# A decoder block's up projection: one 512-column matmul for both parts of x, and banks emptied ahead of weight splits

## The chip, the cores and the metric

The kernel runs on one core of a Trainium2 chip. The metric is the device time of one execution in microseconds (us). Three runs of the kernel before gave 404.71, 404.85 and 405.25 us; the median is 404.85 us.

## What is computed

One decoder block on 256 tokens of width 1024 in float32. The first half normalises x, projects it to q, k, v, an SSM input and two gates, runs attention and a state space model, mixes them and adds the result to x. The second half, where the change lies, is a squared-ReLU MLP:

```python
h = rms_norm(x, norm_mlp_g)
x = x + jnp.square(jax.nn.relu(h @ w_up)) @ w_down    # w_up 1024 x 4096, w_down 4096 x 1024
return rms_norm(x, norm_final_g)
```

## The kernel before, in words

Each float32 operand of a matmul is split in two parts: hi, a copy rounded to the type `F32R`, and lo, the remainder, which is rounded to the same type. A product is then three matmuls, hi·xh, hi·xl and lo·xh; `mm3` (L87 to L90) writes them out. `split` (L82) makes the parts: ScalarE (ACT) writes hi with a copy (L83), VectorE (DVE) writes lo with a subtraction (L84).

Weights come from HBM in units of 128 rows by 1024 columns, 512 KB each. `w_unit` (L73) takes a unit's DMA buffer (tag "raw", 5 buffers) and splits it into tags "hi" and "lo" (4 buffers each). The split is made under a scheduling priority raised by `SPLIT_PRIO` = 800. A planner orders each engine's instructions before the run: what does not depend on each other may change places, and a raised priority lets an instruction go ahead of others that are ready.

The order of stages is: projections, attention and SSM; the GLU (tile `glu`); the output projection (tile `wo`, L676 to L695); the up projection (tile `up`, L705 to L721); the down projection (tiles `dn` and `dnq`, L728 to L796); the final norm.

In the stage `wo`, x is the stationary operand and 512 columns of weights are streamed. It runs over two halves of the channels, c = 0 and 1. Behind each half, DVE adds the residual (L687), TensorE (PE) transposes the result into tile `xt` (L689), ACT writes `x2h` (L693) and DVE writes `x2l` (L694), one 128-channel slice k at a time. Slices k = 0 to 3 come from c = 0, slices 4 to 7 from c = 1.

In the up projection the weights are the stationary operand and the 256 tokens are streamed. One `w_up` unit yields 128 output channels from eight slices k. `up_pair(i)` takes two units, and fills the two halves of one PSUM bank with 2 x 8 x 3 matmuls of 256 columns. It then empties the bank with a Relu on ACT (L714), squares on DVE (L715), and splits the square into `hh` and `hl` (L83 and L84). There are 16 pairs, thus 32 units and 768 matmuls. The banks come from `mm_bank`, a set of three. In the first pair the loop runs over k outside and over the two units inside, in the others the reverse.

Between the two stages, L696 to L699 form the sums of squares of the new x on ACT and turn them into `st2` on DVE. Those are read first by the down projection's `residual` (L739).

Of the kernel before, what the change touches and what calls it, by code (L numbers as in the profile page):

```python
# [8 lines left out]
F32 = mybir.dt.float32  # L9
F32R = mybir.dt.float32r  # L10
BF16 = mybir.dt.bfloat16
I32 = mybir.dt.int32
AF = mybir.ActivationFunctionType
ALU = mybir.AluOpType
PSUM = bass.MemoryType.PSUM

P = 128
D = 1024
T = 256
KD = D // P  # L20
# [3 lines left out]
FF = 4096  # L24
EPS = 1e-6
# [11 lines left out]
SPLIT_PRIO = 800  # L37
HEAT = 7
RSP = 600
ATT_PRIO = 300  # L40
LAST = 4
WQ = (256, 256)
# [6 lines left out]
def build(ctx, tc, dr, out):  # L49
    nc = tc.nc  # L50
    V, S, G, PE = nc.vector, nc.scalar, nc.gpsimd, nc.tensor

    keep = ctx.enter_context(tc.tile_pool(name="keep", bufs=1))
# [4 lines left out]
    def bank(tag, bufs, name):  # L58
        return ps.tile([P, 2, T], F32, tag=tag, bufs=bufs, name=name)

    def mm_bank(name):
        return bank("mm", 3, name)
# [5 lines left out]
    def w_load(src, name):  # L68
        raw = keep.tile([P, 1024], F32, tag="raw", bufs=RAW, name=f"raw_{name}")
        nc.sync.dma_start(raw, src)  # L70
        return raw

    def w_unit(src, name, raw=None):  # L73
        if raw is None:
            raw = w_load(src, name)
        hi = keep.tile([P, 1024], F32R, tag="hi", bufs=HI, name=f"hi_{name}")
        lo = keep.tile([P, 1024], F32R, tag="lo", bufs=LO, name=f"lo_{name}")
        with tc.high_priority(SPLIT_PRIO):
            split(hi, lo, raw)
        return hi, lo  # L80

    def split(hi, lo, x):  # L82
        ins = S.copy(hi, x).ins  # L83
        V.tensor_sub(lo, x, hi.bitcast(F32))  # L84
        return ins

    def mm3(o, wh, wl, xh, xl, first, last, **kw):  # L87
        PE.matmul(o, wh, xh, start=first, stop=False, **kw)  # L88
        PE.matmul(o, wh, xl, start=False, stop=False, **kw)  # L89
        PE.matmul(o, wl, xh, start=False, stop=last, **kw)  # L90
# [28 lines left out]
    for c in range(4):  # L119
# [3 lines left out]
        for k2 in range(2):  # L123
            half = slice(k2 * 512, (k2 + 1) * 512)
# [28 lines left out]
        PE.matmul(hot, heat[:, 0:P], heat, start=True, stop=True)  # L153


    xgh = keep.tile([P, KD, T], F32R, tag="xh", name="xgh")
    xgl = keep.tile([P, KD, T], F32R, tag="xl", name="xgl")
    sq = p1.tile([P, KD, T], F32, tag="yhl", name="sq")
    u_acc = ps.tile([P, 2, 2, T], F32, tag="x", name="u_acc")
    for c in range(4):  # L160
        wh = keep.tile([P, 1024], F32R, tag="hi", bufs=HI, name=f"hi_u{c}")
        wl = keep.tile([P, 1024], F32R, tag="lo", bufs=LO, name=f"lo_u{c}")
        for k2 in range(2):
            k, cols = 2 * c + k2, slice(k2 * 512, (k2 + 1) * 512)
# [12 lines left out]
            ws = [slice(k2 * 512 + m * P, k2 * 512 + (m + 1) * P) for m in range(4)]  # L177
            for i, (w, x) in enumerate(((wh, xgh), (wh, xgl), (wl, xgh))):
                for m in range(4):
                    PE.matmul(u_acc[:, m // 2, m % 2, :], w[:, ws[m]], x[:, k, :],  # L180
                              start=(k == 0 and i == 0 and m % 2 == 0),
                              stop=(k == KD - 1 and i == 2), skip_group_check=True)
# [8 lines left out]
    def rsqrt(eng, dst, m, tmp):  # L191
        V.tensor_scalar(tmp.bitcast(I32), m.bitcast(I32), 1, None, op0=ALU.logical_shift_right)
        V.tensor_scalar(dst.bitcast(I32), tmp.bitcast(I32), -1.0, 1597463007.0,
                        op0=ALU.mult, op1=ALU.add)
        eng.tensor_scalar(m, m, -0.5, None, op0=ALU.mult)
        for _ in range(3):
            eng.tensor_mul(tmp, dst, dst)
            eng.tensor_mul(tmp, tmp, m)
            eng.tensor_scalar(tmp, tmp, 1.5, None, op0=ALU.add)
            eng.tensor_mul(dst, tmp, dst)  # L200

    ms = att_bank("ms")
    for h in range(2):
        for i in range(2):
            PE.matmul(ms[:, 0, h : h + 1], sq[:, i, h * P : (h + 1) * P], ones,
                      start=(i == 0), stop=(i == 1))
# [3 lines left out]
    rs_half = p1.tile([P, 2], F32, name="rs_half")  # L210
    with tc.high_priority(RSP):
        rsqrt(G, rs_tok, rsm[:, 0:2], rsm[:, 4:6])
    V.tensor_scalar(rs_half, rs_tok, 0.5, None, op0=ALU.mult)
    rs_ps = att_bank("rs_ps")
    for h in range(2):
        PE.matmul(rs_ps[:, 0, h * P : (h + 1) * P], rs_tok[:, h : h + 1].to_broadcast([P, P]),
                  ident, start=True, stop=True)
# [52 lines left out]
    def flat(x):  # L270
        return x.rearrange("p a b -> p (a b)")
# [32 lines left out]
    def attn_head(q, k, j):  # L304
        s = att_bank("s").rearrange("p a b -> p (a b)")
        PE.matmul(s[:, 0:128], q[:, j, 0:128], k[:, j, 0:128], start=True, stop=False,
                  skip_group_check=True)
        PE.matmul(s[:, 0:128], ident_b, tri_b, start=False, stop=True, skip_group_check=True)
        PE.matmul(s[:, 128:384], q[:, j, 128:256], k[:, j, :], start=True, stop=False,
                  skip_group_check=True)  # L310
        PE.matmul(s[:, 256:384], ident_b, tri_b, start=False, stop=True, skip_group_check=True)
        st = p1.tile([P, 6], F32, tag="st", bufs=2, name="st")
        V.tensor_reduce(st[:, 0:1], s[:, 0:128], axis=mybir.AxisListType.X, op=ALU.max)
        V.tensor_reduce(st[:, 1:2], s[:, 128:384], axis=mybir.AxisListType.X, op=ALU.max)
        V.tensor_scalar(st[:, 0:2], st[:, 0:2], -scale, None, op0=ALU.mult)
        pr = p1.tile([P, 384], F32, tag="pr", bufs=2, name="pr")
        act(pr[:, 0:128], s[:, 0:128], AF.Exp, bias=st[:, 0:1], scale=scale,
                     accum_out=st[:, 2:3])
        act(pr[:, 128:384], s[:, 128:384], AF.Exp, bias=st[:, 1:2], scale=scale,
                     accum_out=st[:, 3:4])  # L320
        V.reciprocal(st[:, 4:6], st[:, 2:4])
        S.activation(pr[:, 0:128], pr[:, 0:128], AF.Copy, scale=st[:, 4:5])
        S.activation(pr[:, 128:384], pr[:, 128:384], AF.Copy, scale=st[:, 5:6])
        return pr
# [276 lines left out]
    for step in ORDER.split():  # L601
        part, n = step[0], int(step[1])
# [13 lines left out]
        elif part == "S":  # L616
            q, k = qk.pop(n)
            with tc.high_priority(ATT_PRIO):
                prs[n] = [attn_head(q, k, j) for j in range(2)]
# [3 lines left out]
        elif part == "A":  # L623
            with tc.high_priority(ATT_PRIO):
                attn_out(n, prs.pop(n), tha.pop(n))
# [4 lines left out]
        elif part == "B":  # L630
            for i in range(2):
                thb[2 * n + i] = p1.tile([P, 2, T], F32, tag=("cs", "sn")[n], bufs=4,
                                         name=f"thb{2 * n + i}")
# [6 lines left out]
    def wide_banks(name):  # L640
        b = ps.tile([P, 2, 2, T], F32, tag="x", name=name)
        return [flat(b[:, h]) for h in range(2)]

    for q in range(4):
        acc = wide_banks(f"glu{q}") if q % 2 else [flat(mm_bank(f"glu{q}{h}")) for h in range(2)]
        for kk_ in range(2):
            wh, wl = w_unit(dr["w_glu"][2 * q + kk_], f"glu{q}{kk_}")
            for k2 in range(2):
                k, w = 2 * kk_ + k2, slice(k2 * 512, (k2 + 1) * 512)
# [4 lines left out]
        for hf in range(2):  # L654
# [5 lines left out]
            for i in range(2):  # L660
# [3 lines left out]
                               op0=ALU.mult, op1=ALU.add)  # L664
# [4 lines left out]
    p2 = ctx.enter_context(tc.tile_pool(name="ph2", bufs=1))  # L669
    x2t = p2.tile([P, 2, D], F32, name="x2t")  # L670
    nc.sync.dma_start(x2t, dr["x"].rearrange("(h p) d -> p h d", p=P))
    sq2 = p2.tile([P, D], F32, name="sq2")
    st2 = p2.tile([P, 16], F32, name="st2")
    x2h = keep.tile([P, KD, T], F32R, tag="xh", name="x2h")
    x2l = keep.tile([P, KD, T], F32R, tag="xl", name="x2l")
    for c in range(2):  # L676
        acc = wide_banks(f"wo{c}") if c else [flat(mm_bank(f"wo{c}{h}")) for h in range(2)]
        for kk_ in range(4):
            wh, wl = w_unit(dr["w_out"][c, kk_], f"wo{c}{kk_}")
            for k2 in range(2):  # L680
                k, w = 2 * kk_ + k2, slice(k2 * 512, (k2 + 1) * 512)
# [9 lines left out]
        for i in range(4):  # L691
            m, tp = 4 * c + i, tps[i // 2][:, i % 2, :]
            S.activation(x2h[:, m, :], tp, AF.Copy, scale=g_mlp[:, m : m + 1])  # L693
            V.scalar_tensor_tensor(x2l[:, m, :], tp, g_mlp[:, m : m + 1],  # L694
                                   x2h[:, m, :].bitcast(F32), op0=ALU.mult, op1=ALU.subtract)  # L695
    for hf in range(2):  # L696
        S.activation(sq2, x2t[:, hf, :], AF.Square, accum_out=st2[:, hf : hf + 1])
    V.tensor_scalar(st2[:, 2:4], st2[:, 0:2], 1.0 / D, EPS, op0=ALU.mult, op1=ALU.add)
    V.reciprocal(st2[:, 4:6], st2[:, 2:4])  # L699


    hh = p2.tile([P, FF // P, T], F32R, name="hh")
    hl = p2.tile([P, FF // P, T], F32R, name="hl")

    def up_pair(i):  # L705
        acc = mm_bank(f"up{i}")
        ws = [w_unit(dr["w_up"][2 * i + j], f"up{i}{j}") for j in range(2)]
        for k, j in [(k, j) for k in range(KD) for j in range(2)] if i == 0 else \
                    [(k, j) for j in range(2) for k in range(KD)]:
            w = [x[:, k * P : (k + 1) * P] for x in ws[j]]  # L710
            mm3(acc[:, j, :], *w, x2h[:, k, :], x2l[:, k, :],
                k == 0 and (i > 0 or j == 0), k == KD - 1, skip_group_check=(i == 0))
        hr = p2.tile([P, 2, T], F32, tag="hr", bufs=2, name="hr")
        S.activation(hr, acc, AF.Relu)  # L714
        V.tensor_mul(hr, hr, hr)  # L715
        split(hh[:, 2 * i : 2 * i + 2, :], hl[:, 2 * i : 2 * i + 2, :], hr)

    gfin = p2.tile([P, D], F32, name="gfin")
    nc.scalar.dma_start(gfin, dr["gfin"].partition_broadcast(P))
    for i in range(16):  # L720
        up_pair(i)  # L721

    r2 = st2[:, 4:6]
    x3 = x2t
# [43 lines left out]
    for c in range(2):  # L768
        acc = [mm_bank(f"dn{c}{h}").rearrange("p a b -> p (a b)") for h in range(2 - c)]
# [110 lines left out]
```

## Time and profile before

| what | value |
|---|---|
| median of three runs | 404.85 us |
| the profiled execution | 405.1 us |
| its span, first to last instruction | 403.2 us |
| mean granted clock of TensorE, as a share of full speed | 0.995 |
| PE busy share of the span | 98% |
| up projection, first to last matmul | 214.5 to 307.8 us |

The profiled execution takes 1.9 us outside its span. The profile's page gives busy time by engine, then a strip of 40 slices of the span. PE is TensorE's matmuls, PEld its weight loads, DVE VectorE, ACT ScalarE. A matmul's duration overlaps that of the next one, so what a matmul costs in a dense stream is the distance from its start to the start of the next.

### The profile page before, as it was taken

To read this page: it belongs to the slowest core of one execution; us is meant where nothing else is said; L and a number is where in the kernel's file an instruction comes from. 1 tells how busy PE (TensorE), PEld (TensorE's weight loads), DVE (VectorE), ACT (ScalarE), POOL (GpSimd) and SP (SyncE) were. 2 spreads that over 40 slices of the span, in tenths; PEclk is the share of its full clock that TensorE was granted. 3 is DMA by queue.
4 is the path that set the end of the run, shared out by engine and by line. 5 is a ranking of instruction groups with operands and counts; after the bars stand their busy time and mean duration, and the time that the engine had idled before them with its cause. 6 is when DMAs were issued, how large, how long until landed. Compare 5 with 4: busy or idle time off the path is not lost.

```text
span 403.2 us, 6862 instructions
## 1 busy us (share of the span) xinstructions
PE 394.3 (98%) x2635; PEld 355.2 (88%) x2635; DVE 292.8 (73%) x520; ACT 225.9 (56%) x360; POOL 30.3 (8%) x39
## 2 busy tenths in 40 slices
PE   8999999999999999999999999999999999999993
PEld 5988898989899787888889999999999888889983
DVE  5999999999999994769748665656565443564425
ACT  6767977655276557945647645464546334353323
POOL 4151492000000000000000000000000000000000
PEclk9999999999999999999999999999999999999998
DMA  8994843354516252456486465554555565555202
GB/s 228 401 337 149 246 154 102 111 202 151 192 56 208 84 195 102 158 159 206 161 308 209 152 215 191 176 194 172 191 178 193 172 205 169 199 192 178 101 0 104
DMA packets 23199, 71.57 MB, mean 178 GB/s; under 512 B 2944, under 2 KB 5248, under 8 KB 23168
## 3 DMA queue, kind: packets, MB, share of 16 engines
q1 hardware_dynamic: 20144, 68.92, 50.6%
q10 hardware_dynamic: 3024, 2.23, 1.9%
q8 instruction: 20, 0.33, 0.3%
q14 instruction: 11, 0.09, 0.1%
HBM read 69.18 MB, written 1.05 MB: 174 GB/s over the span
## 4 chain that ended last, share of the span: by engine, by line
PE 84%; DVE 5%; DMA 4%; ACT 2%; POOL 2%; issue 1%; ACTq 1%; SPq 0%; DVEq 0%
PE up L89 8%; PE up L90 8%; PE up L88 8%; PE dn L735 6%; PE dn L734 6%; PE dn L733 6%; PE k L88 2%; PE k L89 2%; PE k L90 2%; PE gb L268 2%; PE gb L266 2%; PE gb L267 2%; PE glu L268 2%; PE glu L266 2%; PE dnq L733 2%; PE dnq L735 2%
## 5 line engine op out<-in xcount | busy, mean ns | idle before, releaser
L89 PE MATMUL up<-x2l,hi_up 128*128 128x256 f32 x256 | 72.5, 284 | 0.0
L90 PE MATMUL up<-x2h,lo_up 128*128 128x256 f32 x256 | 72.3, 283 | 0.0
L88 PE MATMUL up<-x2h,hi_up 128*128 128x256 f32 x256 | 71.8, 283 | 0.0
L84 DVE TENSOR_TENSOR lo_dn<-raw_dn,hi_dn 128x1024 fp32r<-128x1024 f32 x32 | 39.2, 1225 | 44.0 <-ACT hi_dn L83 44.0
L83 ACT CAST hi_dn<-raw_dn 128x1024 fp32r<-128x1024 f32 x32 | 33.5, 1048 | 51.6 <-PE dn L735 25.8
L84 DVE TENSOR_TENSOR lo_up<-raw_up,hi_up 128x1024 fp32r<-128x1024 f32 x32 | 38.8, 1223 | 27.7 <-ACT hi_up L83 27.7
L83 ACT CAST hi_up<-raw_up 128x1024 fp32r<-128x1024 f32 x32 | 33.3, 1046 | 39.2 <-PE up L89 18.5
L89 PEld LDWEIGHTS up<-x2l,hi_up 128*128 128x128 f32 x256 | 49.1, 192 | 0.2 <-DVE x2l L694 0.2
L90 PEld LDWEIGHTS up<-x2h,lo_up 128*128 128x128 f32 x256 | 49.1, 192 | 0.0
L88 PEld LDWEIGHTS up<-x2h,hi_up 128*128 128x128 f32 x256 | 48.9, 192 | 0.1
L734 PE MATMUL dn<-lo_dn,hh 128*128 128x512 f32 x96 | 38.0, 395 | 0.0
L735 PE MATMUL dn<-hi_dn,hl 128*128 128x512 f32 x96 | 38.0, 395 | 0.0
L733 PE MATMUL dn<-hi_dn,hh 128*128 128x512 f32 x96 | 37.9, 395 | 0.0
L735 PEld LDWEIGHTS dn<-hi_dn,hl 128*128 128x128 f32 x96 | 18.0, 188 | 4.2
L733 PEld LDWEIGHTS dn<-hi_dn,hh 128*128 128x128 f32 x96 | 18.0, 188 | 3.8
L734 PEld LDWEIGHTS dn<-lo_dn,hh 128*128 128x128 f32 x96 | 18.0, 188 | 3.7
L89 PE MATMUL g<-xgl,hi_g 128*128 128x256 f32 x64 | 18.8, 294 | 0.0
L88 PE MATMUL k<-xgh,hi_k 128*128 128x256 f32 x64 | 18.4, 287 | 0.0
L90 PE MATMUL q<-xgh,lo_q 128*128 128x256 f32 x64 | 18.3, 286 | 0.0
L90 PE MATMUL g<-xgh,lo_g 128*128 128x256 f32 x64 | 18.3, 286 | 0.0
L90 PE MATMUL k<-xgh,lo_k 128*128 128x256 f32 x64 | 18.3, 286 | 0.0
L89 PE MATMUL q<-xgl,hi_q 128*128 128x256 f32 x64 | 18.3, 285 | 0.0
(267 smaller groups left out, 1046.9 us busy)
## 6 DMA issues: line engine op xcount, KB each, us to landing
raw_up<-w_up SPq DMA_DIRECT2D x32, 512.0 KB, 3.4
raw_dn<-w_down SPq DMA_DIRECT2D x32, 512.0 KB, 3.3
raw_v<-w_in SPq DMA_DIRECT2D x8, 512.0 KB, 6.0
raw_q<-w_in SPq DMA_DIRECT2D x8, 512.0 KB, 3.8
raw_k<-w_in SPq DMA_DIRECT2D x8, 512.0 KB, 3.2
raw_g<-w_in SPq DMA_DIRECT2D x8, 512.0 KB, 4.2
raw_gb<-w_in SPq DMA_DIRECT2D x8, 512.0 KB, 3.8
raw_glu<-w_glu SPq DMA_DIRECT2D x8, 512.0 KB, 3.2
```

The costliest lines, as they stand in the source:

```text
L83: ins = S.copy(hi, x).ins
L84: V.tensor_sub(lo, x, hi.bitcast(F32))
L88: PE.matmul(o, wh, xh, start=first, stop=False, **kw)
L89: PE.matmul(o, wh, xl, start=False, stop=False, **kw)
L90: PE.matmul(o, wl, xh, start=False, stop=last, **kw)
L266: PE.matmul(acc, xh[:, k, rows], wh, start=first, stop=False)
L267: PE.matmul(acc, xh[:, k, rows], wl, start=False, stop=False)
L268: PE.matmul(acc, xl[:, k, rows], wh, start=False, stop=last)
L733: PE.matmul(acc, xh, wh[:, w], start=(k == 0), stop=False, skip_group_check=True)
L734: PE.matmul(acc, xh, wl[:, w], start=False, stop=False, skip_group_check=True)
L735: PE.matmul(acc, xl, wh[:, w], start=False, stop=(k == 31), skip_group_check=True)
```

## The change

The two parts of x, until now tiles of their own (`xgh` and `xgl` in the first half, `x2h` and `x2l` in the second), become the two halves of one tile, so that for one k both lie side by side as 512 columns. `up_pair` gives way to `up_group(first, n)`. For each unit and k, one 512-column matmul streams xh and xl through the same hi weights. It puts hi·xh into the first half of a bank and hi·xl into the second half. Eight 256-column matmuls lo·xh follow into the first half. So a unit has 16 matmuls in place of 24, and a bank of its own. To empty it, ACT copies the second half to SBUF and DVE adds the first half; both are put under a priority raised by 2500. For each two units DVE then does ReLU and square in one instruction, and the split into `hh` and `hl` stays. The first call takes three units with k outside and units inside; the other 29 take one unit. The sums of squares move from ahead of the stage to behind its seventh unit.

```diff
+LEAVE_PRIO = 2500
-    xgh = keep.tile([P, KD, T], F32R, tag="xh", name="xgh")
-    xgl = keep.tile([P, KD, T], F32R, tag="xl", name="xgl")
+    xg = keep.tile([P, KD, 2, T], F32R, tag="xhl", name="xg")
+    xgh, xgl = xg[:, :, 0, :], xg[:, :, 1, :]
...
-    x2h = keep.tile([P, KD, T], F32R, tag="xh", name="x2h")
-    x2l = keep.tile([P, KD, T], F32R, tag="xl", name="x2l")
+    x2 = keep.tile([P, KD, 2, T], F32R, tag="xhl", name="x2")
+    x2h, x2l = x2[:, :, 0, :], x2[:, :, 1, :]
...
+    def up_group(first, n):
+        accs = [mm_bank(f"up{first + i}") for i in range(n)]
+        ws = [w_unit(dr["w_up"][first + i], f"up{first + i}") for i in range(n)]
+        for k, i in [(k, i) for k in range(KD) for i in range(n)]:
+            PE.matmul(accs[i].rearrange("p a t -> p (a t)"), ws[i][0][:, k * P : (k + 1) * P],
+                      x2[:, k].rearrange("p a t -> p (a t)"),
+                      start=(k == 0), stop=False, skip_group_check=True)
+        for i, k in [(i, k) for i in range(n) for k in range(KD)]:
+            PE.matmul(accs[i][:, 0, :], ws[i][1][:, k * P : (k + 1) * P], x2h[:, k, :],
+                      start=False, stop=(k == KD - 1), skip_group_check=True)
+        for i in range(n):
+            m = first + i
+            if m % 2 == 0:
+                hs.append(p2.tile([P, 2, T], F32, tag="hs", bufs=2, name="hs"))
+            half = hs[-1][:, m % 2, :]
+            with tc.high_priority(LEAVE_PRIO):
+                S.copy(half, accs[i][:, 1, :])
+                V.tensor_add(half, half, accs[i][:, 0, :])
+            if m % 2:
+                hr = p2.tile([P, 2, T], F32, tag="hr", bufs=2, name="hr")
+                V.scalar_tensor_tensor(hr, hs[-1], 0.0, hs[-1], op0=ALU.max, op1=ALU.mult)
+                split(hh[:, m - 1 : m + 1, :], hl[:, m - 1 : m + 1, :], hr)
...
-    for i in range(16):
-        up_pair(i)
+    up_group(0, 3)
+    for m in range(3, FF // P):
+        up_group(m, 1)
+        if m == 6:
...
```

## Rows read from the trace of the kernel before

**Rows 1.** The page: busy time by engine, and the strip of TensorE's granted clock.
```profile
PE 394.3 (98%) x2635; PEld 355.2 (88%) x2635; DVE 292.8 (73%) x520; ACT 225.9 (56%) x360; POOL 30.3 (8%) x39
...
PEclk9999999999999999999999999999999999999998
```

**Rows 2.** Busy time by stretch, in the stages wo and up.
```profile
core 0: us, PE busy (x) PEld busy (x) DVE busy (x) ACT busy (x) POOL busy (x), PEclk, DMA share, GB/s
...
190.80:212.00 21.20, 21.20 (x99) 17.46 (x98) 12.58 (x17) 11.10 (x13) 0.00 (x0) 1.00 0.63 224
...
226.00:307.90 81.90, 81.90 (x685) 81.90 (x684) 54.56 (x61) 45.32 (x59) 0.00 (x0) 1.00 0.58 194
```

**Rows 3.** Timeline of PE in up: start, duration; 48 steps apart.
```profile
257.11 0.28 PE L88 MATMUL up<-x2h,hi_up 128*128 128x256 f32 x1
...
262.87 0.28 PE L88 MATMUL up<-x2h,hi_up 128*128 128x256 f32 x1
```

**Rows 4.** Timeline of PE in wo, 512 columns; 18 steps apart.
```profile
207.53 0.39 PE L266 MATMUL wo<-hi_wo,mxh 128*128 128x512 f32 x1
...
211.61 0.39 PE L266 MATMUL wo<-hi_wo,mxh 128*128 128x512 f32 x1
```

**Rows 5.** Timeline of PE in dn (512 columns), 17 steps apart.
```profile
329.80 0.39 PE L734 MATMUL dn<-lo_dn,hh 128*128 128x512 f32 x1
...
333.77 0.40 PE L733 MATMUL dn<-hi_dn,hh 128*128 128x512 f32 x1
```

**Rows 6.** Timeline of PE in dnq (256 columns), 10 steps apart.
```profile
356.95 0.28 PE L734 MATMUL dnq<-lo_dn,hh 128*128 128x256 f32 x1
...
358.08 0.28 PE L735 MATMUL dnq<-hi_dn,hl 128*128 128x256 f32 x1
```

**Rows 7.** Groups of instructions: weight splits of up and emptying of its banks.
```profile
L84 DVE TENSOR_TENSOR lo_up<-raw_up,hi_up 128x1024 fp32r<-128x1024 f32 x32 | 38.8, 1223 | 27.7 <-ACT hi_up L83 27.7
...
L83 ACT CAST hi_up<-raw_up 128x1024 fp32r<-128x1024 f32 x32 | 33.3, 1046 | 39.2 <-PE up L89 18.5 <-issue 14.9 <-PE wo L268 4.9
...
L84 DVE TENSOR_TENSOR hl<-hr,hh 128x512 fp32r<-128x512 f32 x16 | 11.0, 685 | 0.0
L715 DVE TENSOR_TENSOR hr<-hr 128x512 f32<-128x512 f32 x16 | 10.9, 683 | 0.0
...
L83 ACT CAST hh<-hr 128x512 fp32r<-128x512 f32 x16 | 9.9, 616 | 0.0
...
L714 ACT ACTIVATE hr<-up 128x512 f32<-128x512 f32 x16 | 9.5, 591 | 0.0
```

**Rows 8.** Groups of instructions: others that read 256 columns of a PSUM bank.
```profile
L693 ACT ACTIVATE x2h<-xt,par 128x256 fp32r<-128x256 f32 x8 | 3.5, 475 | 2.0 <-DVE x2l L694 1.4 <-PE xt L689 0.5
...
L657 DVE SCALAR_TENSOR_TENSOR sg<-sg,glu 128x256 f32<-128x256 f32 x8 | 3.3, 417 | 0.6 <-ACT sg L107 0.5
...
L107 ACT ACTIVATE sg<-glu 128x256 f32<-128x256 f32 x8 | 3.0, 381 | 6.6 <-PE glu L268 4.0 <-DVE sg L657 2.7
```

**Rows 9.** Timeline of PE and PEld at the head of the stage up.
```profile
214.55 0.40 PE L88 MATMUL up<-x2h,hi_up 128*128 128x256 f32 x2
...
214.98 0.19 PEld L89 LDWEIGHTS up<-x2l,hi_up 128*128 128x128 f32 x1 [0.24 <-DVE x2l L694]
```

**Rows 10.** Timeline of PE there, further on.
```profile
218.32 1.03 PE L689 MATMUL xt<-cst,x2t 128*128 128x128 f32 x8
219.11 0.36 PE L89 MATMUL up<-x2l,hi_up 128*128 128x256 f32 x1
```

**Rows 11.** Timeline of ACT there: the first of the two sums of squares.
```profile
216.67 1.06 ACT L697 ACTIVATE sq<-x2t 128x1024 f32<-128x1024 f32 x1
```

**Rows 12.** Timeline of DVE there.
```profile
214.45 0.87 DVE L694 SCALAR_TENSOR_TENSOR x2l<-xt,par,x2h 128x256 fp32r<-128x256 f32 x2
...
217.07 0.47 DVE L694 SCALAR_TENSOR_TENSOR x2l<-xt,par,x2h 128x256 fp32r<-128x256 f32 x1
...
219.47 1.95 DVE L694 SCALAR_TENSOR_TENSOR x2l<-xt,par,x2h 128x256 fp32r<-128x256 f32 x4
```

More of the change, by code (lines that the diff above doesn't have):

```diff
@@ L695, in build @@
                                    x2h[:, m, :].bitcast(F32), op0=ALU.mult, op1=ALU.subtract)
[L696 to L699, printed above, removed]
     hh = p2.tile([P, FF // P, T], F32R, name="hh")
     hl = p2.tile([P, FF // P, T], F32R, name="hl")
[L705 to L716, printed above, removed]
+    def up_group(first, n):
[20 more added lines that the diff above has]
+                split(hh[:, m - 1 : m + 1, :], hl[:, m - 1 : m + 1, :], hr)
@@ L718, in build @@
+    hs = []
     gfin = p2.tile([P, D], F32, name="gfin")
     nc.scalar.dma_start(gfin, dr["gfin"].partition_broadcast(P))
-    for i in range(16):
-        up_pair(i)
+    up_group(0, 3)
+    for m in range(3, FF // P):
+        up_group(m, 1)
+        if m == 6:
+            for hf in range(2):
+                S.activation(sq2, x2t[:, hf, :], AF.Square, accum_out=st2[:, hf : hf + 1])
+            V.tensor_scalar(st2[:, 2:4], st2[:, 0:2], 1.0 / D, EPS, op0=ALU.mult, op1=ALU.add)
+            V.reciprocal(st2[:, 4:6], st2[:, 2:4])
```

## The prediction, made before the changed kernel ran

> **What bounds the kernel now.** I read the page first. TensorE (PE) is busy for 98% of the span, and its granted clock stands at full speed, the higher of its two levels, 2.4 GHz, in all slices but the last [rows 1]. The busy time by stretch says the same of the stage that changes: from 226 to 307.9 us PE and its weight loads are busy without a gap, while DVE has 54.6 and ACT 45.3 us of 81.9 [rows 2]. So the up projection costs what its 768 matmuls take one after the other. A matmul's own duration (0.28 us for 256 columns) overlaps the next, so the price is the step from start to start, and that comes from the timeline:
>
> - up, 256 columns: 5.76 us over 48 steps, 0.1200 us [rows 3].
> - wo, 512 columns: 4.08 us over 18 steps, 0.2267 us [rows 4].
> - dn, 512 columns: 3.97 us over 17 steps, 0.2335 us [rows 5].
> - dnq, 256 columns: 1.13 us over 10 steps, 0.113 us [rows 6].
>
> By the first two, 256 more columns cost 0.1067 us, so a matmul carries 0.0133 us that does not depend on its columns. That is all that fewer, wider matmuls can save.
>
> **The matmuls, the main term.** Per unit and k the change puts one 512-column matmul in place of two 256-column ones; the third stays. Now: 3 x 0.1200 = 0.3600 us. After, by up's and wo's steps: 0.2267 + 0.1200 = 0.3467 us. The saving is 0.0133 us, times 8 k times 32 units = **3.4 us**. No step of a 512-column matmul with weights as the stationary operand is in this trace: wo and dn hold x or the hidden layer there. So both other rows are bounds. With dn's 0.2335 and up's 0.1200 the pair costs 0.3535 us and the saving is 1.7 us. With wo's 0.2267 and dnq's 0.113 it costs 0.3397 us and the saving is 5.2 us. I take 3.4, for two reasons. It joins a size measured in this very stage, on these very operands, with the stage just ahead of it. And dn with dnq, taken as a pair, give 0.3465 us, the same sum.
>
> The Trainium skill, "TensorE: Matmul & The Clock Gate", section "Back-to-back issue gap", gives a warm step as columns over 2.4 GHz plus 2.5 ns. By it the step of 256 columns would be 109 ns and of 512 columns 216 ns, and the saving 2.5 ns x 256 = 0.6 us. The steps of 0.1200 and 0.2267 us here are both some 11 ns longer than that rule, so the trace doesn't bear it out.
>
> **Emptying a bank.** Before, a pair takes a Relu of 0.591, a hi split of 0.616 on ACT, a square of 0.683 and a lo split of 0.685 on DVE [rows 7]. After, the two copies on ACT read 256 columns of PSUM each: the rows of that shape are 0.381 and 0.475 [rows 8]. The two adds on DVE are nearest to a row of 0.417 [rows 8]. ReLU and square in one instruction of 512 columns I price at 0.683, as the square; both splits stay. With two weight splits per pair (1.046 ACT, 1.223 DVE [rows 7]) and a pair every 5.55 us:
>
> - ACT: 2 x 1.05 + 2 x 0.38 to 0.48 + 0.62 = 3.5 to 3.7 us, 66% at most.
> - DVE: 2 x 1.22 + 2 x 0.42 + 0.68 + 0.69 = 4.65 us, 84% (now 3.8 of 5.76, 66%).
>
> Neither becomes the bound. A unit's bank is wanted again three units later, so there are two units, 5.5 us, for an emptying of about 0.4 + 0.45 us and the handovers. Raising it above the weight splits puts a copy that waits for PE ahead of split casts on ACT's queue, and an add ahead of lo splits on DVE's. Queued behind them are the splits of later units, and PE waits for those. But ACT's casts wait now for PE to let go of a buffer (18.5 us in all [rows 7]): the splits run as far ahead as four buffers allow, three units or 8 us. A copy that blocks them for a part of a unit is covered. If that cover were gone, each 0.1 us per unit would cost 3.2 us. I take nothing for the steady stretch.
>
> **DMA.** 512 KB each 2.77 us are 189 GB/s. The stretch now runs at 194, and wo at 224 [rows 2]. Nothing.
>
> **Sums of squares.** Two instructions of 1.06 us leave the head of the stage on ACT [rows 11], where `x2h` of slices 4 to 7 queued behind them, with two small DVE ones. They issue no DMA. They land in ACT's slack of some 0.9 us per unit, and their reader is `residual` behind the first half of dn, over 100 us later. Nothing; PE hardly waited for `x2h` before either.
>
> **The head of the stage, the one loss.** Today PE starts on xh alone at 214.55, and waits 0.24 us for the first xl [rows 9]. A 512-column matmul needs both parts. The first `x2l` is done near 214.9, so PE waits some 0.38 us: 0.14 more. Slice 3 comes at 217.07 + 0.47 = 217.54, and slices 4 to 7 from 219.47 on at 0.49 us each [rows 12]. Three units' slices 0 to 3 are 12 x 0.2267 = 2.7 us of work, their lo·xh matmuls 12 x 0.1200 = 1.4 us, the transposes 0.8 us [rows 10]. From 214.93 that lasts until 219.9, just enough, if the planner lets lo·xh go ahead of slices 4 to 7 (it traded places likewise before: the second pair was begun ahead of the transposes). Then the three banks of the first call fill nearly together and no fourth is free. The last call on the first bank is about 8 steps, 0.96 us, ahead of the group's end. The path to a free bank is the matmul's own 0.28, a copy of 0.4, an add of 0.42 and handovers of some 0.15 us, 1.25 us in all: PE waits 0.2 us. If a cast or lo split just started stands in the way of ACT or DVE (1.05, 1.22), it waits up to 1.4 us. In all the head loses 0.2 to 1.6 us; I take **0.8**, since both engines have splits to do just then, as the hi buffers come free.
>
> **The first half.** The q, k, v and gate matmuls read the same slices at other addresses, one tile instead of two. As many instructions, the same shapes. I price it at nothing, with 0.5 us either way for a different order.
>
> **The sum.** Against the profiled execution's own time, 405.1 (span 403.2 and 1.9 outside it): 405.1 - 3.4 + 0.8 = 402.5. That execution is 0.25 above the median of the runs, so the forecast is **402.25**, 2.6 us or 0.6% below 404.85.
>
> **Rivals.**
> - A, the forecast: 402.25, by the loss at the head 401.65 to 403.05. Chance 0.53.
> - B, 512 columns at dn's step, 256 at up's: saving 1.7 less 0.8, 403.95 (403.35 to 404.75). For it: dn has the same type and shape. Against: dnq's smaller step belongs to the same stage. Chance 0.11.
> - C, 512 columns at wo's step, 256 columns at dnq's: saving 5.2 less 0.8, 400.45. For it: the wider matmul leaves longer for the next weight load. Against: up's 0.1200 is on the same operands. Chance 0.08.
> - D, the head in the order as written, lo·xh behind all slices: PE waits 0.57 for slice 3 and 0.86 for slice 4, and with the 0.14 some 1.6 us, up to 2.5 with the banks: 403.05 to 403.95, I give 403.5. Against: today's order is already interleaved. Chance 0.09.
> - E, fewer instructions hardly save, as the fixed part is not a price per matmul but of the stage: 0.6 less 0.8, 405.05. That is the skill's rule quoted above, worked as a mechanism. Against: two sizes in two stages leave the same remainder. Chance 0.06.
> - F, slower: the second 256 columns cost what dn pays over dnq, 0.2335 - 0.113 = 0.1205, so that 512 columns of x2 take 0.1200 + 0.1205 = 0.2405 us. The main term becomes -0.1 us and the head's 0.8 stays: 405.8. It decides from a 512-column step of 0.2369 us on, where saving and loss are equal. For it: dn streams slower than wo, and I see no row that says why. Chance 0.10.
> - G, the first half shifts by half a microsecond and more: chance 0.03, both signs.
>
> **How the numbers follow.** A difference of 0.2%, 0.8 us, is about what a measurement of this kernel tells from none: below 404.04 is faster, above 405.66 slower. Faster: A, C, most of D (0.07), half of B (0.05) and a part of G, 0.74. Same: the rest of B and D, E, some of G, 0.15. Slower: F and a part of G, 0.11. The range from 400.6 to 404.8 takes in A, B, D and half of C, and leaves out E, F and the rest, 0.2.
>
> **What would show it.** In the changed trace: the step of the 512-column matmul in up (0.2267; 0.2335 for B; 0.2405 for F) and of the 256-column one (0.1200; 0.113 for C); Relu gone, and from one unit's copy to the next's 2.77 us; PE gaps at the head of 0.4 us before the first matmul and up to 1.4 us at the fourth unit; after that none. Wrong would be this: PE waiting for DVE in the steady stretch, a step of DVE above 84%, or a first half that is not the same to half a microsecond.

## The result, and the profile of the changed kernel

The changed kernel takes 406.77 us, the kernel before 404.89 us in the same runs. The ratio is 1.0055, 95% interval 1.0038 to 1.0073: slower by 1.9 us, where 2.6 us less was forecast. The profiled execution takes 406.64 us, its span is 404.8 us. The up projection runs from 214.14 us to the first matmul of `dn` at 309.54, 95.40 us; before it ran from 214.55 to 307.86, 93.31 us. What follows the stage takes 95.3 us in both, and what stands ahead of it ends 0.4 us earlier here, so the loss of 2.1 us lies inside this stage.

The page's busy shares hardly tell anything, against [rows 1]:

```profile
PE 393.6 (97%) x2379; PEld 342.7 (85%) x2379; DVE 305.1 (75%) x552; ACT 226.7 (56%) x376; POOL 30.2 (7%) x39
...
PEclk9999999999999999999999899999999999999998
```

But the strip of the granted clock has an 8 in the middle of the span. The timeline of PE (start, duration, and in brackets the idle time before and who ended it) shows the head of the stage, where [rows 9] and [rows 10] stood:

```profile
214.14 2.21 PE L709 MATMUL up<-x,hi_up 128*128 128x512 f32 x9
216.19 1.03 PE L690 MATMUL xt<-cst,x2t 128*128 128x128 f32 x8
216.98 0.94 PE L709 MATMUL up<-x,hi_up 128*128 128x512 f32 x3
218.60 3.36 PE L709 MATMUL up<-x,hi_up 128*128 128x512 f32 x12 [0.68 <-DVE x L695]
221.80 3.03 PE L713 MATMUL up<-x,lo_up 128*128 128x256 f32 x24
226.89 2.52 PE L709 MATMUL up<-x,hi_up 128*128 128x512 f32 x8 [2.06 <-DVE hs L722]
```

PE waits twice: 0.68 us for the later slices of x, and 2.06 us before the fourth unit (226.89) for `hs`, the add that empties the first bank. Counted from start to start, with three hi steps (0.68 us) and 24 lo steps of 0.12 (2.88 us) taken off, these cost 0.94 and 2.21 us. Merged rows hide waits of 0.1 to 0.2 us: the 12 hi steps from 218.60 on take 3.20 us where 12 of 0.230 (the steady step of this stage, eight in the 1.84 us from 256.47 to 258.31 below) make 2.76, so the later slices cost another 0.44 us. The timelines of ACT and of DVE at that place show what stood in the way of the emptying:

```profile
215.34 1.06 ACT L737 ACTIVATE sq<-x2t 128x1024 f32<-128x1024 f32 x1
...
217.57 0.82 ACT L694 ACTIVATE x<-xt,par 128x256 fp32r<-128x256 f32 x2
...
221.55 2.94 ACT L84 CAST hi_up<-raw_up 128x1024 fp32r<-128x1024 f32 x3 [2.10 <-PE up L709]
224.40 0.91 ACT L721 COPY hs<-up 128x256 f32<-128x256 f32 x3
```

```profile
223.01 3.50 DVE L85 TENSOR_TENSOR lo_up<-raw_up,hi_up 128x1024 fp32r<-128x1024 f32 x3 [3.04 <-ACT hi_up L84]
226.42 1.08 DVE L722 TENSOR_TENSOR hs<-hs,up 128x256 f32<-128x256 f32 x3
```

The first bank is full near 222.9 (seven lo steps and one duration behind 221.80). Its copy starts at 224.40, behind three casts, and its add at 226.42, behind three lo splits. And the sums of squares are still at the head, at 215.34, ahead of the x slices 4 and 5 at 217.57. Then PE's timeline, further on:

```profile
229.22 1.91 PE L713 MATMUL up<-x,lo_up 128*128 128x256 f32 x8
230.92 2.42 PE L709 MATMUL up<-x,hi_up 128*128 128x512 f32 x8
...
234.12 2.00 PE L709 MATMUL up<-x,hi_up 128*128 128x512 f32 x8
...
256.47 2.00 PE L709 MATMUL up<-x,hi_up 128*128 128x512 f32 x8
258.31 1.11 PE L713 MATMUL up<-x,lo_up 128*128 128x256 f32 x8
259.26 2.00 PE L709 MATMUL up<-x,hi_up 128*128 128x512 f32 x8
```

In the steady stretch a unit takes 2.79 us (256.47 to 259.26), 0.09 less than before. The fourth and fifth units take 7.23 us together (226.89 to 234.12) in place of 5.59: 1.64 us more. The busy time by stretch tells why; the number after POOL is the granted clock:

```profile
227.00:228.00 1.00, 1.00 (x5) 0.82 (x6) 1.00 (x3) 0.00 (x0) 0.00 (x0) 1.00 1.01 205
228.00:229.00 1.00, 1.00 (x5) 0.82 (x4) 0.31 (x2) 0.62 (x1) 0.00 (x0) 0.69 1.00 283
229.00:230.00 1.00, 1.00 (x5) 0.90 (x5) 0.48 (x1) 0.55 (x1) 0.00 (x0) 0.50 0.86 352
230.00:231.00 1.00, 1.00 (x7) 1.00 (x6) 0.00 (x0) 0.50 (x1) 0.00 (x0) 0.50 0.52 213
231.00:232.00 1.00, 1.00 (x4) 0.79 (x4) 0.78 (x1) 0.37 (x1) 0.00 (x0) 0.60 0.00 0
232.00:233.00 1.00, 1.00 (x6) 0.80 (x5) 0.97 (x3) 0.00 (x0) 0.00 (x0) 1.00 0.00 0
```

From about 228.4 to 231.8 us the clock is granted at the lower of its two levels, 1.2 GHz, although PE works again. So the theory: 0.94 + 0.44 + 2.21 + 1.64 = 5.23 us are lost at the head, where the kernel before lost 0.36 (its 93.31 us less 768 steps of 0.12 and 0.79 for the transposes). The wide matmuls gain 2.77 us over the stage (0.0865 us in each of 32 units). That leaves a loss of 2.10 us, as measured. Its rivals: the emptying path itself is too long; the wide matmuls cost more than reckoned; the raised priority does it.

### The profile page after: what moved, and what is told of

Its sections match the earlier page's. It is cut to its first block, busy times and chain, and to the rows that moved or that the text cites. A ratio compares the mean times of both kernels' runs of the same rounds, so it can differ in the third digit from the quotient of the medians.

```text
span 404.8 us, 6384 instructions
## 1 busy us (share of the span) xinstructions
PE 393.6 (97%) x2379; PEld 342.7 (85%) x2379; DVE 305.1 (75%) x552; ACT 226.7 (56%) x376; POOL 30.2 (7%) x39
## 3 DMA queue, kind: packets, MB, share of 16 engines
HBM read 69.18 MB, written 1.05 MB: 173 GB/s over the span
## 4 chain that ended last, share of the span: by engine, by line
PE 82%; DVE 5%; ACT 4%; DMA 4%; POOL 2%; issue 2%; ACTq 1%; SPq 0%; DVEq 0%
PE up L709 14%; PE up L713 8%; PE dn L753 6%; PE dn L752 6%; PE dn L751 6%; PE k L89 2%; PE k L90 2%; PE k L91 2%; PE gb L269 2%; PE gb L267 2%; PE gb L268 2%; PE glu L269 2%; PE dnq L751 2%; PE glu L267 2%; PE glu L268 2%; PE dnq L753 2%
## 5 line engine op out<-in xcount | busy, mean ns | idle before, releaser
L709 PE MATMUL up<-x,hi_up 128*128 128x512 f32 x256 | 65.5, 397 | 2.8 <-DVE hs L722 2.1
L709 PEld LDWEIGHTS up<-x,hi_up 128*128 128x128 f32 x256 | 46.5, 191 | 12.2 <-DVE hs L722 2.3
L713 PEld LDWEIGHTS up<-x,lo_up 128*128 128x128 f32 x256 | 35.5, 195 | 2.5
L713 PE MATMUL up<-x,lo_up 128*128 128x256 f32 x256 | 36.2, 286 | 0.0
L90 PE MATMUL g<-xg,hi_g 128*128 128x256 f32 x64 | 18.8, 294 | 0.0
L89 PE MATMUL k<-xg,hi_k 128*128 128x256 f32 x64 | 18.4, 287 | 0.0
L91 PE MATMUL q<-xg,lo_q 128*128 128x256 f32 x64 | 18.3, 286 | 0.0
L91 PE MATMUL g<-xg,lo_g 128*128 128x256 f32 x64 | 18.3, 286 | 0.0
L91 PE MATMUL k<-xg,lo_k 128*128 128x256 f32 x64 | 18.3, 286 | 0.0
L90 PE MATMUL q<-xg,hi_q 128*128 128x256 f32 x64 | 18.3, 285 | 0.0
L89 PE MATMUL g<-xg,hi_g 128*128 128x256 f32 x64 | 18.3, 285 | 0.0
L90 PE MATMUL k<-xg,hi_k 128*128 128x256 f32 x64 | 18.2, 284 | 0.0
```

The lines of the kernel that those rows point to most:

```text
L709: PE.matmul(accs[i].rearrange("p a t -> p (a t)"), ws[i][0][:, k * P : (k + 1) * P], x2[:, k].rearrange("p a t -> p (a t)"), start=(k == 0 ...
L713: PE.matmul(accs[i][:, 0, :], ws[i][1][:, k * P : (k + 1) * P], x2h[:, k, :], start=False, stop=(k == KD - 1), skip_group_check=True)
```

## The experiments

Ratios are to the kernel before, run beside each kernel on the same chip. "Stage" is from the first matmul of `up` to the first of `dn` in the profiled execution (93.31 before, 95.40 changed). An order is forced with `behind`, the kernel's own helper: it tells the planner which of two instructions of an engine comes first, and adds no wait.

### Empty the first banks ahead of the splits

```diff
-        ws = [w_unit(dr["w_up"][first + i], f"up{first + i}") for i in range(n)]
+        ws = [w_unit(dr["w_up"][first + i], f"up{first + i}", None,
+                     left if 4 <= first <= 6 else None) for i in range(n)]
...
+            behind(ins, after[0])     # cast of units 4 to 6: behind the three copies
+            behind(sub, after[1])     # lo split of units 4 to 6: behind the three adds
```

> Splits of units 4 to 6 are ordered behind the emptying of the first three banks, on ACT and on DVE; nothing else changes. Theory 1 (the changed kernel loses its gain at the fourth unit: the banks of the first call are emptied behind three casts and three lo splits, PE waits 2.06 us, and the granted clock then falls to half for some 3.5 us, which costs unit 3 and 4 another 1.66 us): the wait falls below 0.4 us, the clock stays at full speed, and the time is 3.3 to 3.7 us below the changed kernel's 406.8, 403.1 to 403.5. Rival 2 (it is the emptying path itself, matmul, copy and add, with three banks filled together): PE still waits 1 us or more, 404.5 to 406. Rival 3 (512-column matmuls cost more than reckoned over the whole stage): no change, 406.5 and more.

Measured: 403.83 us, 0.9966 (0.9951 to 0.9981); the stage takes 92.01 us. The timeline of PE, with the same two rows as above, now without a wait at the fourth unit (226.60):

```profile
220.53 3.38 PE L713 MATMUL up<-x,hi_up 128*128 128x512 f32 x12 [0.69 <-DVE x L698]
223.74 3.03 PE L717 MATMUL up<-x,lo_up 128*128 128x256 f32 x24
226.60 2.00 PE L713 MATMUL up<-x,hi_up 128*128 128x512 f32 x8
228.44 1.11 PE L717 MATMUL up<-x,lo_up 128*128 128x256 f32 x8
```

On ACT the copies now stand ahead of the three casts:

```profile
224.89 0.37 ACT L725 COPY hs<-up 128x256 f32<-128x256 f32 x1 [3.52 <-PE up L717]
...
227.07 2.95 ACT L84 CAST hi_up<-raw_up 128x1024 fp32r<-128x1024 f32 x3
```

The wait and the fall of the clock are gone, with three banks filled together as before. So the path itself is short enough, and the splits in front of it are the cause. The median lies 0.3 us above the expected 403.1 to 403.5, but on this chip the kernel before also takes 0.3 us more, 405.21; the ratio gives 403.5.

### Hold the sums of squares

```diff
...
-                S.activation(sq2, x2t[:, hf, :], AF.Square, accum_out=st2[:, hf : hf + 1])
+                behind(S.activation(sq2, x2t[:, hf, :], AF.Square,
+                                    accum_out=st2[:, hf : hf + 1]).ins, [left])   # the 7th unit's copy
```

> The sums of squares are held behind the seventh unit's copy on ACT. In the changed kernel they still run at 215.34 to 217.6 us, ahead of slices 4 to 7 of xh, and PE waits 0.68 us for slice 4. Theory 1: that wait ends or falls under 0.2 us, the wait of 2.06 us and the fall of the clock stay, 406.0 to 406.4. Rival: slice 4 is late because of the lo split of unit 3 on DVE, the wait stays and the time with it, 406.8.

Measured: 406.97 us, 1.0046 (1.0022 to 1.0070), stage 93.25 us. The timeline of PE:

```profile
217.70 4.25 PE L709 MATMUL up<-x,hi_up 128*128 128x512 f32 x15
221.79 3.03 PE L713 MATMUL up<-x,lo_up 128*128 128x256 f32 x24
226.89 2.12 PE L709 MATMUL up<-x,hi_up 128*128 128x512 f32 x8 [2.06 <-DVE hs L722]
...
232.59 2.00 PE L709 MATMUL up<-x,hi_up 128*128 128x512 f32 x8
```

The wait of 0.68 us is gone, the second stands to the hundredth. So the two have separate causes. Short waits for the slices remain: the 15 hi steps from 217.70 take 4.09 us where 15 of 0.230 make 3.45. So holding the squares wins some 0.7 of the 1.4 us that the later slices cost. The time can't be told from the changed kernel's, and the forecast of 406.0 to 406.4 was missed: the intervals overlap, and 0.4 us lie between the ratios. In this profiled execution the clock did not fall, though the wait was the same. The fourth and fifth units take 5.70 us (226.89 to 232.59), 0.11 more than two steady ones. So of the 1.64 us behind the wait in the changed kernel, 1.53 go with the fall of the clock.

### All units singly

```diff
-    up_group(0, 3)
-    for m in range(3, FF // P):
+    up_group(0, 1)
+    for m in range(1, FF // P):
```

> No call with three units: all 32 units singly. Theory 1: the banks fill one after another, 1.2 us apart, and fewer casts stand ahead of the first copy; PE waits under 0.8 us at the fourth unit, the clock doesn't fall, 403 to 404. Rival 2 (the path itself): a wait of 1 us and more stays, 404.5 to 406. Rival 3: 406.5 and more.

Measured: 403.95 us, 0.9970 (0.9950 to 0.9989), stage 92.03 us. The planner still mixes the first three units over the slices, but it ends each with its eight lo matmuls before the next, so that the banks fill 1.2 us apart. Then the plan puts one split between two emptyings, not three ahead of all. PE doesn't wait at the fourth unit. The wait for slices 4 to 7 stays, at 0.69 us.

### Without the raised priority

```diff
-            with tc.high_priority(LEAVE_PRIO):
-                S.copy(half, accs[i][:, 1, :])
-                V.tensor_add(half, half, accs[i][:, 0, :])
+            S.copy(half, accs[i][:, 1, :])
+            V.tensor_add(half, half, accs[i][:, 0, :])
```

> The changed kernel without the raised priority for emptying a bank. Theory 1 (the raise changes nothing: at the moment ACT and DVE are free in the plan, the copy and the add are not ready yet, so there is no choice to make): every engine's order is the changed kernel's, PE waits 2.06 us at the fourth unit, 0.4% to 0.7% above the kernel before. Rival (the raise moves the emptying and is part of the loss or of the gain): another order of casts and copies, and a time more than 0.2% off the changed kernel's.

Measured: 407.44 us, 1.0058 (1.0041 to 1.0076). In the trace the order of work on every engine is the changed kernel's, instruction for instruction; PE waits 2.06 us, and the clock falls again (0.50 from 230 to 232 us). This half of the change does nothing at all. The reason is argued, not shown: if a raised priority decides only between instructions that are ready at the same moment, it has no say here, because the splits of units 4 to 6 are ready first.

### Fill the wait with matmuls

```diff
...
+        if first == 3:
+            waste = att_bank("waste")
+            for i in range(16):    # behind the third unit's last lo matmul; its result is not used
+                behind(PE.matmul(waste[:, 0, :], ws[0][0][:, 0:P], x2h[:, i % KD, :],
+                                 start=(i == 0), stop=(i == 15), skip_group_check=True).ins, tail)
...
```

> Behind the third unit PE does 16 more matmuls of 256 columns (1.92 us, result not used), so that it works while the banks are emptied; when the banks come free doesn't change. Theory 1 (the wait of 2.06 us itself lets the granted clock fall in some or all executions, which costs up to 1.66 us more): full clock in the stretch from 226 to 236 us, the fourth unit starts at the same distance behind the third (some 2.1 us, 0.3 at most more), and the time is 0.7 to 1.7 us below that of the kernel without the raised priority. Rival (the fall has nothing to do with the wait): the same time as that kernel, or a fall all the same.

Measured: 405.98 us, 1.0027 (1.0015 to 1.0039), 1.46 us less than the kernel without the raised priority on the same chip. PE's timeline:

```profile
222.34 3.04 PE L718 MATMUL up<-x,lo_up 128*128 128x256 f32 x24
225.21 2.08 PE L711 MATMUL waste<-x,hi_up 128*128 128x256 f32 x16
227.43 2.14 PE L714 MATMUL up<-x,hi_up 128*128 128x512 f32 x8
229.41 1.10 PE L718 MATMUL up<-x,lo_up 128*128 128x256 f32 x8
230.34 2.00 PE L714 MATMUL up<-x,hi_up 128*128 128x512 f32 x8
```

The fourth unit starts 2.22 us behind the end of the third (225.21 to 227.43), as in the changed kernel (2.21). Nothing was gained there. But the granted clock is 1.00 in every stretch from 209 to 236 us, and a kernel with 16 useless matmuls is faster. So PE's idle time lets the clock fall, and the fall costs about 1.5 us, as the 1.53 read from the traces. The mean granted clock of all executions of the two kernels points the same way: half the clock for 3.4 us takes 0.004 from it, and it is 0.996 or more in ten of the eleven with the useless matmuls, and 0.992 or less in four of the five of the kernel without the raised priority.

### Both waits taken away

One kernel joins the first two edits, another the second and third.

> Splits of units 4 to 6 behind the emptying of the first three banks, and the sums of squares behind the seventh unit's copy. Theory 1 (the head's two waits, 0.68 and 2.06 us, are the whole loss, and each has its own cause): neither wait is there, the stage from its first matmul to the first of dn takes 91.2 to 91.5 us (93.35 before), and the time is 0.45% to 0.6% below the kernel before. Rival (taking one wait away moves it to another place): the stage takes 92 us or more.

> All 32 units singly, and the sums of squares behind the seventh unit's copy. Theory 1: as with the other one, no wait for a bank and none for slice 4, the stage takes 91.2 to 91.5 us, 0.45% to 0.6% below the kernel before. Rival: with one bank after the other instead of three together, PE has less to do while slices 4 to 7 are made, and waits 0.3 us or more for them; stage 91.7 us or more.

Measured: 402.75 us, 0.9946 (0.9928 to 0.9963), stage 91.25 us, for the first; 402.62 us, 0.9950 (0.9931 to 0.9968), stage 90.82 us, for the second. The timeline of PE in the second:

```profile
217.34 3.81 PE L709 MATMUL up<-x,hi_up 128*128 128x512 f32 x13
220.98 1.11 PE L713 MATMUL up<-x,lo_up 128*128 128x256 f32 x8
221.93 0.40 PE L709 MATMUL up<-x,hi_up 128*128 128x512 f32 x1
222.17 1.12 PE L713 MATMUL up<-x,lo_up 128*128 128x256 f32 x8
...
224.32 2.00 PE L709 MATMUL up<-x,hi_up 128*128 128x512 f32 x8
```

No wait for a bank is left, and either way gives the same time. The slices are still waited for in short pieces. In the second kernel the 13 hi steps from 217.34 take 3.64 us where 13 of 0.230 make 2.99, so 0.65 us remain; the changed kernel's stage of 95.40 less the 5.23 us of the theory is 90.17, and 90.82 were measured. The first kernel has 0.64 us of the same, and 0.44 more among its first nine steps (2.51 us to the transposes at 216.91, where nine of 0.230 make 2.07):

```profile
214.40 2.68 PE L713 MATMUL up<-x,hi_up 128*128 128x512 f32 x9 [0.25 <-DVE x L698]
```

That is the difference between the two stages. It is not the edit's: those nine steps take from 2.05 to 2.52 us in the profiled executions of the kernels that begin with nine wide steps, and 2.05 and 2.18 us in two executions of one and the same kernel. Both kernels beat the changed kernel and the kernel before. A second run of the one with single units, on another chip, gave the same:

> The kernel without waits at the head, on the same chip, to compare: 0.4% to 0.6% below the kernel before.

Measured: 402.99 us, 0.9954 (0.9938 to 0.9970), stage 90.96 us.

### Undo the width

```diff
-            PE.matmul(accs[i].rearrange("p a t -> p (a t)"), ws[i][0][:, k * P : (k + 1) * P],
-                      x2[:, k].rearrange("p a t -> p (a t)"),
-                      start=(k == 0), stop=False, skip_group_check=True)
+            for h, x in enumerate((x2h, x2l)):
+                PE.matmul(accs[i][:, h, :], ws[i][0][:, k * P : (k + 1) * P], x[:, k, :],
+                          start=(k == 0 and h == 0), stop=False, skip_group_check=True)
```

First in the changed kernel, then in the one with single units and held squares.

> The changed kernel with two 256-column matmuls in place of each 512-column one; banks, emptying and first call as they are. Theory 1 (the wide matmul saves 0.0865 us per unit, 2.880 less 2.793): a unit takes 2.88 us again, and the time is some 2.5 us above the changed kernel's, 409.0 to 409.6. Rival 3 (it saves nothing, or costs): 406.8 or less, the unit's step at 2.79.

> The kernel without waits at the head (all units singly, squares held) with two 256-column matmuls in place of each 512-column one: only the width is undone, and no fall of the clock blurs it. Theory 1 (the width saves 0.0865 us per unit in the steady stretch): a unit takes 2.88 us, the stage 93.6 to 94.0 us, the time within 0.25% of the kernel before, some 2.5 us above the one with wide matmuls. Rival (the gain of that kernel comes from the new head, not from the width): 0.4% below the kernel before, like that one.

Measured: 408.57 us, 1.0078 (1.0056 to 1.0100), and 405.71 us, 1.0020 (1.0004 to 1.0036). The first lies only 0.9 us above the changed kernel by the ratios, not 2.5: its profiled execution has the wait of 2.06 us and no fall of the clock, so a loss that comes and goes blurs the comparison. The second has no wait for a bank, and it is 0.70%, 2.8 us, above the same kernel with wide matmuls. Its stage takes 94.44 us, more than the 93.6 to 94.0 expected: in this execution PE also waits some 0.9 us for the first slices, 21 steps from 214.97 to 218.41 taking 3.44 us in place of 2.52. So the price of the width is better read from the unit, which takes 2.88 us (257.57 to 260.45):

```profile
214.97 0.51 PE L710 MATMUL up<-x,hi_up 128*128 128x256 f32 x3
215.86 2.72 PE L710 MATMUL up<-x,hi_up 128*128 128x256 f32 x18 [0.38 <-DVE x L695]
218.41 1.04 PE L690 MATMUL xt<-cst,x2t 128*128 128x128 f32 x8
...
257.57 2.08 PE L710 MATMUL up<-x,hi_up 128*128 128x256 f32 x16
259.49 1.12 PE L713 MATMUL up<-x,lo_up 128*128 128x256 f32 x8
260.45 1.72 PE L710 MATMUL up<-x,hi_up 128*128 128x256 f32 x13
```

So the width is worth 0.09 us per unit, 2.8 us over 32 units, and the new head alone, without it, is no gain.

### Alternate the two widths

```diff
-        for i, k in [(i, k) for i in range(n) for k in range(KD)]:
             PE.matmul(accs[i][:, 0, :], ws[i][1][:, k * P : (k + 1) * P], x2h[:, k, :],
```

The lo matmul of a slice comes right behind its hi matmul: in all units, and then from the fourth unit on only.

> The kernel without waits at the head, with the eight lo matmuls of a unit each right behind the hi matmul of its slice, so that steps of 512 and 256 columns alternate. Theory 1 (the pair of steps costs 0.349 us however they are ordered): a unit takes 2.79 us, the time 0.45% to 0.6% below the kernel before. Rival (a row of 512-column matmuls costs more each, 0.230 in place of wo's 0.2267, because weight loads are waited for; alternating, the pair costs 0.3467 or less): a unit takes 2.77 us or less, the stage 0.6 us shorter.

> The kernel without waits at the head, hi and lo matmuls alternating from the fourth unit on only, so that the first three banks still fill 1.2 us apart. Theory 1 (alternating saves 0.023 us per unit, and the loss of the kernel that alternates throughout was the bank wait and the clock at its head): a unit takes 2.77 us, PE doesn't wait at the fourth, the stage takes 90.4 to 90.8 us, and the time is 0.6 us below the kernel without alternation, 0.55% to 0.75% below the kernel before. Rival (alternating holds the hi buffers to a unit's end, and splits come late): waits for splits in the steady stretch, no better than 0.5%.

Measured: 406.09 us, 1.0023 (1.0007 to 1.0038), and 403.80 us, 0.9975 (0.9964 to 0.9986). The first has the shorter step that the rival expected, eight pairs in 2.77 us:

```profile
256.00 0.39 PE L709 MATMUL up<-x,hi_up 128*128 128x512 f32 x1
...
258.77 0.39 PE L709 MATMUL up<-x,hi_up 128*128 128x512 f32 x1
```

But it is slower, because the planner alternated over the first three units too. Their banks filled together again, and the old loss came back whole, with the clock at half speed behind it:

```profile
226.58 0.78 PE L709 MATMUL up<-x,hi_up 128*128 128x512 f32 x1 [1.92 <-DVE hs L721]
```

The second has no wait for a bank, as its theory said, but misses the time: 0.25% below the kernel before where 0.55% to 0.75% were expected, and a stage of 91.83 us. Its pairs take longer, seven in 2.47 us, 0.353 us each instead of 0.346:

```profile
255.87 0.40 PE L712 MATMUL up<-x,hi_up 128*128 128x512 f32 x1
...
258.34 0.40 PE L712 MATMUL up<-x,hi_up 128*128 128x512 f32 x1
```

From the fourth unit on both issue the same matmuls in the same order. Why one steps at 0.346 us and the other at 0.353 is open. So alternating is no improvement that could be relied on.

## Why the prediction was wrong, point by point

- **What bounds the kernel**: right. PE's steps set the stage, before and after.
- **The main term**, 3.4 us: right in kind, somewhat too large. The pair of steps costs 0.349 us in the changed kernel (2.79 us over eight), where 0.3467 was worked out: 0.0865 us per unit, 2.8 us in all. The eight 512-column steps take 1.84 us, 0.230 each, between wo's 0.2267 and dn's 0.2335, the two rows that were given as bounds. Rival F, a step of 0.2405, didn't come. The step rule quoted from the Trainium skill ("TensorE: Matmul & The Clock Gate", "Back-to-back issue gap"), which that section gives for an isolated matmul, would by the prediction's estimate have let the width save 0.6 us; 0.0865 us in each of 32 units make 2.8 us, so the measurement stands against it here.
- **The head, 0.8 us (0.2 to 1.6; rival D up to 2.5)**: this step failed. The head lost 5.2 us, 4.9 more than before. Three things in it were wrong. First, it let the planner move the lo matmuls ahead of slices 4 to 7, as it had moved the second pair; it left them behind, as rival D had it, and the later slices cost 1.4 us. D was given 0.09; its waits for slices 3 and 4, 0.57 and 0.86 (0.95 by the rows it takes them from), were near. Second, the wait for a bank was priced with one cast or split in the way, 1.05 and 1.22 us. There were three of each, because the three hi buffers of the first call come free at the same moment, 2.9 us ahead of the last lo matmul: all three casts are ready before any bank is full, and a copy behind them waits for them: that of the bank full near 222.9 began at 224.40. PE lost 2.21 us. This wait doesn't hang on the first point: in the kernel that alternates throughout, the lo matmuls do stand among the slices and the squares are held. From its first matmul to the last lo matmul of its third unit 9.1 us pass (215.25 to 224.39), 9.0 of them work, and PE still waits 1.92 us for the bank. Third, what a wait does to the clock was not priced at all; it cost 1.53 us in the changed kernel's trace. [rows 1] shows a clock at full level in a kernel that never lets PE idle for 2 us, and can't tell what happens to one that does.
- **Emptying a bank, the steady stretch**: right. PE never waits for a bank behind the fourth unit. The copy takes 0.367 and the add 0.415 us, against 0.38 to 0.48 and 0.42 that were taken from [rows 8]; DVE is busy 63.1 of 81.9 us where 54.6 stood in [rows 2].
- **The raised priority**: costed at nothing, and that is what it does, which was luck: it was said to put copies ahead of casts, with the buffers as cover, and it changes no order at all.
- **The sums of squares**: costed at nothing because they would leave the head. They didn't leave it. To write them further down did not move them: the planner still put them where ACT was free and their operands were there; they kept 2.2 us of ACT in front of slices 4 to 7. Before, that was hidden by 24 matmuls that needed only the first slices and a second pair behind them [rows 10]; with the new order they cost some 0.7 us, the part of the 1.4 us for the later slices that went when they were held.
- **DMA, the first half**: no loss, as forecast.

## What to carry to other kernels

When one call fills several buffers at once, all that frees them is queued at once too: price the wait with everything that becomes ready in that moment on each in-order engine, not with one instruction. Here neither the raised priority nor the later place in the program moved anything; what had to come later needed an explicit order. And a wait on a PE that had none may be paid twice: add what the granted clock can take away behind it.

## What the runs showed of the hardware that was not expected

- A wait of some 2 us on PE (1.92 to 2.06) was followed, in three of five profiled executions that have it, by a stretch at half the granted clock (0.50 in the rows), in the changed kernel from 1.5 us behind the end of the wait and for 3.4 us. The two others kept full clock. With 2.08 us of useless matmuls in the wait, it stayed at 1.00.
- A 512-column step is not one number. With the same operand shapes it was 0.2267 us in wo, 0.2335 in dn, 0.230 in the changed stage, and a pair with a 256-column step was 0.346 or 0.353 us in two kernels that issue the same order.
